# Half-array products of a decoder trunk gathered into longer sequences on TensorE

## The chip, the cores and the metric

The kernel runs on one core of a Trainium2 chip, written in Bass with the Tile framework. The metric is the device time of one execution in microseconds (us), the median over several runs. The engines are named as in the profile: PE is TensorE (matrix products; PEld is its weight load), DVE is VectorE, ACT is ScalarE, POOL is GpSimd, SP is SyncE, which issues the DMAs. PE multiplies with an array of 128 x 128 cells. A product that contracts over 64 rows, or that has 64 output columns, uses half of it.

## What is computed

Two layers of a decoder trunk over 256 positions of width 1024, in float32. Each layer normalizes x, projects it with `w_in`, runs three groups of heads next to each other, joins them with one output projection, adds the residual, and then does the same with a SwiGLU feed-forward network (FFN). The parts that the change touches are the retention (6 heads of width 64, chunks of 128 positions) and the weighted values of the sparse attention (NSA, 6 heads):

```python
def retention(q, k, v, g):
    ...
    scores = jnp.einsum('bhcnd,bhcmd->bhcnm', qc, kc) * decay[:, None]
    inner = jnp.einsum('bhcnm,bhcme->bhcne', scores, vc)
    ...
    o = rms_norm(o) * jax.nn.silu(g.astype(f32))

# nsa: compressed, selected and window branch, each a softmax over its keys
        o_c = jnp.einsum('bghqn,bgnd->bghqd', p_c, v_cmp)
        o_s = jnp.einsum('bghqk,bgqkd->bghqd', p_s, vs)
        o_w = jnp.einsum('bghqk,bgkd->bghqd', p_w, vw)
        return g[..., 0:1] * o_c + g[..., 1:2] * o_s + g[..., 2:3] * o_w

    x = x + (mix @ w_out[l])
```

## The kernel before

**Precision.** The large projections run as three products in the format fp32r: every weight piece comes by DMA into a staging tile `wst` (3 of them), ACT casts it to `whi` (6 tiles), and DVE subtracts that from the original to give `wlo` (6 tiles). A piece of `whi` and `wlo` is free again when PE has used it last; only then can the next cast into it begin, and a `wst` tile is free for the next DMA when its `wlo` is made. Small products in the heads are plain fp32; each stands in the trace as two records of PE.

**The order of work.** The kernel is written as threads (Python generators) that yield operations, wait for events or ask a pool for a tile. A planner, `Desk`, runs the threads against assumed costs while the program is built, and always issues the request that can start first, with priorities among those that can. The order that comes out is fixed: every engine works through its own instructions in that order, and an instruction whose inputs are not ready holds up all that stand behind it on the same engine. A list of operations yielded at once is issued without anything else of that engine between them.

**Pools.** PSUM has 8 banks: four `acc` for the projections and four `sm` for everything small (transposes, scores, sums). `S` has 4 tiles in SBUF for weighted scores.

**A layer, in order.** The projection is done in seven parts (`nk`, `nq`, `gm`, `nv`, `rq`, `rk`, `rg`), and the heads' threads start as their parts are done, so their small products are mixed in between the records of the later parts (`acc<-whi,hcat` and `acc<-wlo,hcat`, 384 columns wide in the last part, `rg`, the gate of the retention).

- Weighted values, `pv` (L1059): a thread for each j of 3, each with the two heads of both key groups g. It waits for the values `Vt`, the compressed probabilities `pcT` and the four softmax units that it uses, takes one `sm` bank, and yields 9 products: one of the compressed branch (`sm<-pcT,vbd`, 96 rows, full array), then 8 with 64 output columns each (`sm<-PT,V`, half of the array by columns; the two of g = 0 and 1 go to the two halves). Then `split` casts the bank on ACT (`nsh`) and subtracts on DVE (`nsl`).
- Retention, `retention` (L1159): three threads `scores(p)`, one for each pair of heads. Each takes two `S` tiles and two `sm` banks and yields two lists of two products that contract over 64 rows (`sm<-qkT`, half of the array by rows; the two heads lie on the two halves), 256 and 128 columns wide. For each head DVE then multiplies both parts with the decay (`S<-sm,cst`). The main thread takes, head by head, the 6 products of that head's sums (`sm<-rv,S`, 64 output columns, half of the array by columns) into two `sm` banks.
- `ret_norm` (L1209) squares the sums on ACT (`w2k<-sm`), reduces them on DVE, takes the inverse root by Ln and Exp on ACT, and scales (`ro`); `rg_tile` (L1222) multiplies with Silu of the gate, transposes on PE (`sm<-cst,ro`) and splits the result into `rth` and `rtl`. Silu and Ln/Exp need different tables of ACT.
- The output projection, `residual` (L1366), uses gm, then ns, then rt operands (`acc<-whi,gmh`, ..., `acc<-whi,rth`).

In the rows L196 is the line of the helper that records every operation, so operations are told apart by their tiles.

Of the kernel before, what the change touches and what calls it, by code (L numbers as in the profile page):

```python
# [258 lines left out]
class Desk:  # L259
# [33 lines left out]
    def give(self, pool, item):  # L293
        self.given += 1
        pool.free.append((self.cur.t, self.given, item))
        self._serve(pool)
# [94 lines left out]
class Trunk:  # L391
# [479 lines left out]
    def mix_nv(self, l, ps):  # L871
        self.gx = self.tiny("gx", [128, 2, 18])
        for t in range(2):
            self.desk.fork(self.nv_tile(l, t, ps[t]), 12)
        self.desk.fork(self.gates(l), 11)
        self.desk.fork(self.compress(l), 14)
        for h in range(0, 6, 2):
            self.desk.fork(self.unit(0, h), 18)
        for h in (0, 3, 1, 4, 2, 5):
            self.desk.fork(self.unit(1, h), 16)  # L880
        for j in range(3):
            self.desk.fork(self.pv(l, j), 9)

    def nv_tile(self, l, t, ps):
        V, A = self.V, self.A
# [22 lines left out]
    def compress(self, l):  # L908
# [6 lines left out]
        for j in range(2):  # L915
# [33 lines left out]
            self.vmask[:, :, None].to_broadcast([96, 6, 64]), op=ALU.mult,  # L949
        )  # L950
        give(self.sm, pv)

        pk = yield Need(self.sm)
# [102 lines left out]
        for i in range(m):  # L1056
            self.desk.fire(self.ev_u[t, h + i])

    def pv(self, l, j):  # L1059

        for t in range(2):
            yield self.ev_v[t]
        yield self.ev_pc
        for t in range(2):
            for g in range(2):
                yield self.ev_u[t, 3 * g + j]
        mm = self.PE.matmul
        po = yield Need(self.sm)
        ops = [
            mm(  # L1070
                po[:, :256], self.vbd[:, 2 * j : 2 * j + 2, :].rearrange("p g d -> p (g d)"), self.pcT,
                start=True, stop=False,
            )
        ]
        for b in range(2):
            for kt in range(2):
                qs = slice(128 * kt, 256)
                ks = slice(0, 256) if kt == 0 else slice(256, 384)
                for g in range(2):
                    vs = slice(b * 128 + g * 64, b * 128 + g * 64 + 64)  # L1080
                    ops.append(
                        mm(
                            po[64 * g : 64 * g + 64, qs], self.Vt[kt][:, vs], self.PT[:, 6 * b + 3 * g + j, ks],
                            start=False, stop=b == 1 and kt == 1,
                        )
                    )
        yield ops
        yield from self.split(self.nsh[j], self.nsl[j], po[:, :256])
        self.desk.give(self.sm, po)
        self.desk.fire(self.ev_ns[j])  # L1090


    def rope(self, src, dst, nh, t):
# [65 lines left out]
    def retention(self, l):  # L1159
        PE, V, give = self.PE, self.V, self.desk.give  # L1160
        for t in range(2):
            for e in (self.ev_rq[t], self.ev_rk[t], self.ev_rv[t][0], self.ev_rv[t][1]):
                yield e
        at = {}
        done = [Event() for _ in range(6)]


        def scores(p):
            yield self.ev_dec
            heads = []  # L1170
            for r in (0, 64):
                at[2 * p + r // 64] = a = yield Need(self.S)
                ps = yield Need(self.sm)
                heads.append((a, ps, self.qkT[r : r + 64, 3 + p, :], self.qkT[r : r + 64, p, :]))
            yield [PE.matmul(ps[:, :256], kT[:, :128], qT, start=True, stop=True) for _, ps, kT, qT in heads]
            yield [
                PE.matmul(ps[:, 256:384], kT[:, 128:], qT[:, 128:], start=True, stop=True) for _, ps, kT, qT in heads
            ]
            for h, (a, ps, _, _) in zip((2 * p, 2 * p + 1), heads):
                yield [  # L1180
                    V.tensor_tensor(a[:, :256], ps[:, :256], self.dec[:, h, :], op=ALU.mult),
                    V.tensor_tensor(a[:, 256:384], ps[:, 256:384], self.dec[:, h, :128], op=ALU.mult),
                ]
                give(self.sm, ps)
                self.desk.fire(done[h])

        for p in range(3):
            self.desk.fork(scores(p))
        po = []
        for h in range(6):  # L1190
            yield done[h]
            if h == 0:
                for t in range(2):
                    p = yield Need(self.sm)
                    po.append(p)
            hs = slice(h * 64, h * 64 + 64)
            a = at[h]
            yield [
                PE.matmul(
                    po[q][r : r + 64, hs], a[:, c + r : c + r + 64], self.rv[k][:, hs], start=k == 0, stop=k == q  # L1200
                )
                for q, k, c in ((0, 0, 0), (1, 0, 128), (1, 1, 256))
                for r in (0, 64)
            ]
            give(self.S, a)
        for t in range(2):
            self.desk.fork(self.ret_norm(t, po[t]))

# [407 lines left out]
```

## Time and profile before

| | us |
|---|---|
| median of 3 runs | 645.78 (645.46 to 646.02) |
| the profiled execution, its own time | 646.46 |
| its span, first to last instruction | 644.70 |
| PE busy | 635.1 (99%) |
| DVE busy | 452.9 (70%) |
| ACT busy | 364.8 (57%) |
| DMA, from HBM | 109.64 MB, 172 GB/s over the span |

A busy PE in this profile is one with a record open; records overlap in the pipeline, so the share says that PE was given work without a break, and the distance between the starts of neighbouring records says how fast it went. The chain that ended last lies on PE for 89% of the span and on DMAs for 5%.

### The profile page before, as it was taken

To read this page: it belongs to the slowest core of one execution; us is meant where nothing else is said; L and a number is where in the kernel's file an instruction comes from. 1 tells how busy PE (TensorE), PEld (TensorE's weight loads), DVE (VectorE), ACT (ScalarE), POOL (GpSimd) and SP (SyncE) were. 2 spreads that over 40 slices of the span, in tenths; PEclk is the share of its full clock that TensorE was granted. 3 is DMA by queue.
4 is the path that set the end of the run, shared out by engine and by line. 5 is a ranking of instruction groups with operands and counts; after the bars stand their busy time and mean duration, and the time that the engine had idled before them with its cause. 6 is when DMAs were issued, how large, how long until landed. Compare 5 with 4: busy or idle time off the path is not lost.

```text
span 644.7 us, 9955 instructions
## 1 busy us (share of the span) xinstructions
PE 635.1 (99%) x3628; PEld 533.6 (83%) x3628; DVE 452.9 (70%) x1046; ACT 364.8 (57%) x685; POOL 11.0 (2%) x28
## 2 busy tenths in 40 slices
PE   8979999999999999999999999999999999999998
PEld 7768887788888888888887888788888888888886
DVE  5867988488677677664388899865867677776441
ACT  7648963576456555543377795444755555545330
POOL 0120000000000000010000000000000000000000
PEclk9999999999999999999999999999999999999999
DMA  8885245157555565566546522534665556565631
GB/s 257 284 228 175 91 123 181 66 166 231 190 180 192 185 196 192 185 257 204 163 135 196 196 92 64 173 110 149 186 191 185 193 195 187 174 197 184 192 114 65
DMA packets 32816, 111.63 MB, mean 173 GB/s; under 512 B 4339, under 2 KB 4851, under 8 KB 32512
## 3 DMA queue, kind: packets, MB, share of 16 engines
q1 hardware_dynamic: 32256, 109.86, 52.4%
q0 software_dynamic: 512, 1.14, 0.9%
q8 instruction: 28, 0.46, 0.3%
q14 instruction: 20, 0.16, 0.1%
HBM read 109.64 MB, written 1.35 MB: 172 GB/s over the span
## 4 chain that ended last, share of the span: by engine, by line
PE 89%; DMA 5%; ACT 2%; DVE 2%; issue 1%; SPq 0%; ACTq 0%
PE acc L196 60%; PE sm L196 29%; DMA wst<-in_wts_dram 5%; ACT whi L196 1%; DVE wlo L196 1%; DMA x<-in_x_dram 1%; DVE x L196 0%; SPq L196 0%; ACT w2k L196 0%; ACT L402 0%; ACT L196 0%; DVE Kl L196 0%; ACT Kh L196 0%; ACT hcat L196 0%; ACT w1k L196 0%
## 5 line engine op out<-in xcount | busy, mean ns | idle before, releaser
L196 DVE TENSOR_TENSOR wlo<-wst,whi 128x1024 fp32r<-128x1024 f32 (+3 forms) x204 | 245.0, 1202 | 140.8 <-ACT whi L196 139.6
L196 ACT CAST whi<-wst 128x1024 fp32r<-128x1024 f32 (+3 forms) x204 | 209.2, 1028 | 195.0 <-issue 49.7
L196 PE MATMUL acc<-whi,hcat 128*128 128x512 f32 (+2 forms) x512 | 141.2, 381 | 0.0
L196 PEld LDWEIGHTS acc<-whi,hcat 128*128 128x128 f32 x512 | 91.6, 189 | 15.0 <-issue 0.7
L196 PE MATMUL acc<-hcat,whi 128*128 128x512 f32 x320 | 101.2, 396 | 0.0
L196 PE MATMUL sm<-hcat,whi 128*128 128x512 f32 x320 | 99.7, 392 | 0.0
L196 PE MATMUL acc<-wlo,hcat 128*128 128x512 f32 (+2 forms) x256 | 80.6, 381 | 0.0
L196 PEld LDWEIGHTS sm<-hcat,whi 128*128 128x128 f32 x320 | 60.0, 188 | 14.2
L196 PEld LDWEIGHTS acc<-hcat,wlo 128*128 128x128 f32 x320 | 58.8, 188 | 11.7
L196 PE MATMUL sm<-hcat,wlo 128*128 128x256 f32 x320 | 64.4, 282 | 0.0
L196 PE MATMUL acc<-hcat,wlo 128*128 128x256 f32 x320 | 64.1, 282 | 0.0
L196 PEld LDWEIGHTS acc<-wlo,hcat 128*128 128x128 f32 x256 | 46.8, 189 | 7.8 <-issue 0.3
L196 PEld LDWEIGHTS acc<-hcat,whi 128*128 128x128 f32 x320 | 50.9, 190 | 1.7
L196 PE MATMUL acc<-whi,ah 128*128 128x512 f32 (+1 forms) x176 | 50.0, 378 | 0.0
L196 PE MATMUL acc<-whi,al 128*128 128x512 f32 (+1 forms) x176 | 50.0, 378 | 0.0
L196 PE MATMUL acc<-wlo,ah 128*128 128x512 f32 (+1 forms) x176 | 49.9, 377 | 0.0
L196 PEld LDWEIGHTS sm<-hcat,wlo 128*128 128x128 f32 x320 | 49.6, 190 | 0.0
L196 PEld LDWEIGHTS acc<-whi,ah 128*128 128x128 f32 x176 | 31.9, 188 | 5.5
L196 PEld LDWEIGHTS acc<-wlo,ah 128*128 128x128 f32 x176 | 31.8, 188 | 5.5
L196 PEld LDWEIGHTS acc<-whi,al 128*128 128x128 f32 x176 | 31.8, 188 | 5.5
L196 ACT ACTIVATE hcat<-sm,par 128x128 fp32r<-128x128 f32 x64 | 18.6, 379 | 9.2 <-PE sm L196 9.2
L196 DVE SCALAR_TENSOR_TENSOR hcat<-sm,par,hcat 128x128 fp32r<-128x128 f32 x64 | 18.5, 344 | 4.5 <-ACT hcat L196 4.5
(212 smaller groups left out, 726.6 us busy)
## 6 DMA issues: line engine op xcount, KB each, us to landing
wst<-in_wts_dram SPq DMA_DIRECT2D x186, 512.0 KB, 3.8
wst<-in_wts_dram SPq DMA_DIRECT2D x8, 384.0 KB, 3.0
w<-in_w_dram SPq DMA_DIRECT2D x2, 1024.0 KB, 7.0
wst<-in_wts_dram SPq DMA_DIRECT2D x4, 411.0 KB, 4.4
x<-in_x_dram SPq DMA_DIRECT2D x4, 256.0 KB, 5.3
wst<-in_wts_dram SPq DMA_DIRECT2D x4, 256.0 KB, 3.3
cst<-in_cst_dram SPq DMA_DIRECT2D x1, 768.0 KB, 5.3
B<-scr POOLq DMA_DIRECT2D x4, 192.0 KB, 6.2
```

The costliest lines, as they stand in the source:

```text
L196: return Op(self.name, lambda: fn(*a, **k), dur, table, lat, prio, banks)
```

## The change

`mix_nv` starts one thread `pv(l)` in place of three. It waits for all twelve units, takes three `sm` banks, and yields the three full-array products of the compressed branch in one list, and then three lists of 8 half-array products with a priority ahead of all other work; a small thread `finish(j)` splits each bank when its list is done. `retention` issues the scores of the first two pairs in one list, then, when all four heads have been multiplied with the decay, the scores of the third pair and the sums of heads 0 to 3 in one list, and then the sums of heads 4 and 5. The wait for the decay table moves ahead of it all. What is computed, and with which products, stays as it was.

```diff
@@ -878,8 +878,7 @@
             self.desk.fork(self.unit(0, h), 18)
         for h in (0, 3, 1, 4, 2, 5):
             self.desk.fork(self.unit(1, h), 16)
-        for j in range(3):
-            self.desk.fork(self.pv(l, j), 9)
+        self.desk.fork(self.pv(l), 9)
 
     def nv_tile(self, l, t, ps):
         V, A = self.V, self.A
@@ -1056,38 +1055,55 @@
         for i in range(m):
             self.desk.fire(self.ev_u[t, h + i])
 
-    def pv(self, l, j):
+    def pv(self, l):
+
 
         for t in range(2):
             yield self.ev_v[t]
         yield self.ev_pc
         for t in range(2):
-            for g in range(2):
-                yield self.ev_u[t, 3 * g + j]
+            for h in range(6):
+                yield self.ev_u[t, h]
         mm = self.PE.matmul
-        po = yield Need(self.sm)
+        pos = []
+        for j in range(3):
+            po = yield Need(self.sm)
+            pos.append(po)
         ops = [
             mm(
-                po[:, :256], self.vbd[:, 2 * j : 2 * j + 2, :].rearrange("p g d -> p (g d)"), self.pcT,
-                start=True, stop=False,
+                pos[j][:, :256], self.vbd[:, 2 * j : 2 * j + 2, :].rearrange("p g d -> p (g d)"), self.pcT,
+                start=True, stop=False, lat=False,
             )
+            for j in range(3)
         ]
-        for b in range(2):
-            for kt in range(2):
-                qs = slice(128 * kt, 256)
-                ks = slice(0, 256) if kt == 0 else slice(256, 384)
-                for g in range(2):
-                    vs = slice(b * 128 + g * 64, b * 128 + g * 64 + 64)
-                    ops.append(
-                        mm(
-                            po[64 * g : 64 * g + 64, qs], self.Vt[kt][:, vs], self.PT[:, 6 * b + 3 * g + j, ks],
-                            start=False, stop=b == 1 and kt == 1,
+        yield ops
+        done = [Event() for _ in range(3)]
+
+        def finish(j):
+            yield done[j]
+            yield from self.split(self.nsh[j], self.nsl[j], pos[j][:, :256])
+            self.desk.give(self.sm, pos[j])
+            self.desk.fire(self.ev_ns[j])
+
+        for j in range(3):
+            self.desk.fork(finish(j))
+        for j in range(3):
+            ops = []
+            for b in range(2):
+                for kt in range(2):
+                    qs = slice(128 * kt, 256)
+                    ks = slice(0, 256) if kt == 0 else slice(256, 384)
+                    for g in range(2):
+                        vs = slice(b * 128 + g * 64, b * 128 + g * 64 + 64)
+                        ops.append(
+                            mm(
+                                pos[j][64 * g : 64 * g + 64, qs], self.Vt[kt][:, vs],
+                                self.PT[:, 6 * b + 3 * g + j, ks],
+                                start=False, stop=b == 1 and kt == 1, lat=False, prio=-2,
+                            )
                         )
-                    )
-        yield ops
-        yield from self.split(self.nsh[j], self.nsl[j], po[:, :256])
-        self.desk.give(self.sm, po)
-        self.desk.fire(self.ev_ns[j])
+            yield ops
+            self.desk.fire(done[j], self.desk.LAT["PE"])
 
 
     def rope(self, src, dst, nh, t):
@@ -1161,21 +1177,25 @@
         for t in range(2):
             for e in (self.ev_rq[t], self.ev_rk[t], self.ev_rv[t][0], self.ev_rv[t][1]):
                 yield e
+        yield self.ev_dec
         at = {}
         done = [Event() for _ in range(6)]
 
 
-        def scores(p):
-            yield self.ev_dec
+        def open_pair(p):
             heads = []
             for r in (0, 64):
                 at[2 * p + r // 64] = a = yield Need(self.S)
                 ps = yield Need(self.sm)
                 heads.append((a, ps, self.qkT[r : r + 64, 3 + p, :], self.qkT[r : r + 64, p, :]))
-            yield [PE.matmul(ps[:, :256], kT[:, :128], qT, start=True, stop=True) for _, ps, kT, qT in heads]
-            yield [
+            return heads
+
+        def scores(heads):
+            return [PE.matmul(ps[:, :256], kT[:, :128], qT, start=True, stop=True) for _, ps, kT, qT in heads] + [
                 PE.matmul(ps[:, 256:384], kT[:, 128:], qT[:, 128:], start=True, stop=True) for _, ps, kT, qT in heads
             ]
+
+        def decay(p, heads):
             for h, (a, ps, _, _) in zip((2 * p, 2 * p + 1), heads):
                 yield [
                     V.tensor_tensor(a[:, :256], ps[:, :256], self.dec[:, h, :], op=ALU.mult),
@@ -1184,25 +1204,47 @@
                 give(self.sm, ps)
                 self.desk.fire(done[h])
 
-        for p in range(3):
-            self.desk.fork(scores(p))
+        def sums(heads):
+            for h in heads:
+                hs = slice(h * 64, h * 64 + 64)
+                for q, k, c in ((0, 0, 0), (1, 0, 128), (1, 1, 256)):
+                    for r in (0, 64):
+                        yield PE.matmul(
+                            po[q][r : r + 64, hs], at[h][:, c + r : c + r + 64], self.rv[k][:, hs],
+                            start=k == 0, stop=k == q,
+                        )
+
+        first = yield from open_pair(0)
+        second = yield from open_pair(1)
+        yield scores(first) + scores(second)
+        self.desk.fork(decay(0, first))
+        self.desk.fork(decay(1, second))
+        for h in range(4):
+            yield done[h]
+        third = []
+        ps3 = []
+        for r in (0, 64):
+            ps = yield Need(self.sm)
+            ps3.append(ps)
         po = []
-        for h in range(6):
+        for t in range(2):
+            p = yield Need(self.sm)
+            po.append(p)
+        third = [
+            (None, ps, self.qkT[r : r + 64, 5, :], self.qkT[r : r + 64, 2, :]) for r, ps in zip((0, 64), ps3)
+        ]
+        yield scores(third) + list(sums(range(4)))
+        for h in range(4):
+            give(self.S, at[h])
+        for i, h in enumerate((4, 5)):
+            at[h] = yield Need(self.S)
+            third[i] = (at[h], *third[i][1:])
+        self.desk.fork(decay(2, third))
+        for h in (4, 5):
             yield done[h]
-            if h == 0:
-                for t in range(2):
-                    p = yield Need(self.sm)
-                    po.append(p)
-            hs = slice(h * 64, h * 64 + 64)
-            a = at[h]
-            yield [
-                PE.matmul(
-                    po[q][r : r + 64, hs], a[:, c + r : c + r + 64], self.rv[k][:, hs], start=k == 0, stop=k == q
-                )
-                for q, k, c in ((0, 0, 0), (1, 0, 128), (1, 1, 256))
-                for r in (0, 64)
-            ]
-            give(self.S, a)
+        yield list(sums((4, 5)))
+        for h in (4, 5):
+            give(self.S, at[h])
         for t in range(2):
             self.desk.fork(self.ret_norm(t, po[t]))
 
```

What this does to the order shows at three places. First PE in layer 0 at the weighted values, as a piece of the difference between the two programs (`V_0_131` and `V_0_132` are the values of the two halves of the positions):

```order
 L196 MATMUL acc_64<-wlo_83,hcat 128x384
 L196 MATMUL sm_68<-pcT_135,vbd_134 128x256
+L196 MATMUL sm_67<-pcT_135,vbd_134 128x256
+L196 MATMUL sm_70<-pcT_135,vbd_134 128x256
 L196 MATMUL sm_68<-PT_133,V_0_131 64x256 x2
 L196 MATMUL sm_68<-PT_133,V_0_132 64x128 x2
 L196 MATMUL sm_68<-PT_133,V_0_131 64x256 x2
 L196 MATMUL sm_68<-PT_133,V_0_132 64x128 x2
-L196 MATMUL sm_67<-pcT_135,vbd_134 128x256
 L196 MATMUL sm_67<-PT_133,V_0_131 64x256 x2
 L196 MATMUL sm_67<-PT_133,V_0_132 64x128 x2
```

The second full-array product moves from between two half-array strings to ahead of them; the third does the same.

Second PE in layer 1, in the retention: the sums of heads 0 to 2 before, each head between full-array products of the gate's projection or scores (`acc`; one `S` tile for each head).

```order
L196 MATMUL sm_67<-rv_1_2929,S_1_2935 64x64 x2
L196 MATMUL sm_69<-rv_1_2929,S_1_2935 64x64 x2
L196 MATMUL sm_69<-rv_1_2930,S_1_2935 64x64 x2
L196 MATMUL acc_63<-whi_76,hcat 128x384
L196 MATMUL acc_64<-whi_76,hcat 128x384
L196 MATMUL sm_67<-rv_1_2929,S_1_2936 64x64 x2
L196 MATMUL sm_69<-rv_1_2929,S_1_2936 64x64 x2
L196 MATMUL sm_69<-rv_1_2930,S_1_2936 64x64 x2
L196 MATMUL acc_63<-whi_77,hcat 128x384
L196 MATMUL acc_64<-whi_77,hcat 128x384
```

And the same heads on PE after the change, which follow the third pair's scores:

```order
L196 MATMUL sm_69<-qkT_2931 128x128
L196 MATMUL sm_70<-qkT_2931 128x128
L196 MATMUL sm_68<-rv_1_2929,S_1_2935 64x64 x2
L196 MATMUL sm_67<-rv_1_2929,S_1_2935 64x64 x2
L196 MATMUL sm_67<-rv_1_2930,S_1_2935 64x64 x2
L196 MATMUL sm_68<-rv_1_2929,S_1_2936 64x64 x2
L196 MATMUL sm_67<-rv_1_2929,S_1_2936 64x64 x2
L196 MATMUL sm_67<-rv_1_2930,S_1_2936 64x64 x2
L196 MATMUL sm_68<-rv_1_2929,S_1_2937 64x64 x2
L196 MATMUL sm_67<-rv_1_2929,S_1_2937 64x64 x2
```

The gate's products have gone from between the heads: 16 of them now stand between the first scores and the third, 10 between the sums of heads 0 to 3 and those of 4 and 5, and 8 behind these.

Third ACT in layer 1, from the squares of the sums (`w2k<-sm`) to the retention's result (`rth`). Before:

```order
L196 ACTIVATE w2k_91<-sm_67 128x384
L196 ACTIVATE w2k_92<-sm_69 128x384
L196 CAST whi_77<-wst_74 128x1024
L196 ACTIVATE rtr_z<-rtr_ss 128x6 x2
L196 ACTIVATE rtr_y<-rtr_z 128x6
L196 CAST whi_78<-wst_75 128x1024
L196 ACTIVATE rtr_y<-rtr_z 128x6
L196 CAST whi_79<-wst_73 128x1024
L196 ACT_TABLE_LOAD
L196 ACTIVATE w2k_89<-acc_63,rstd_110 128x384
L196 ACTIVATE w2k_90<-acc_64,rstd_111 128x384
```

After:

```order
L196 ACTIVATE w2k_88<-sm_68 128x384
L196 ACTIVATE w2k_92<-sm_67 128x384
L196 CAST whi_79<-wst_73 128x1024
L196 ACTIVATE rtr_z<-rtr_ss 128x6 x2
L196 ACT_TABLE_LOAD
L196 ACTIVATE w2k_93<-acc_63,rstd_110 128x384
L196 ACTIVATE w2k_90<-acc_64,rstd_111 128x384
L402 ACT_TABLE_LOAD
L196 ACTIVATE rtr_y<-rtr_z 128x6 x2
```

Silu of the gate (`w2k<-acc,rstd`) and its table now stand between Ln (`rtr_z`) and Exp (`rtr_y`), with a second table load; a further one follows at the start of layer 1's FFN, as the table is no longer that of Silu there. In layer 0 Silu moves the other way, ahead of the squares.

## Rows read from the trace of the kernel before

**Rows 1.** The page's first part: busy time of each engine in us (share of the span) x instructions.

```profile
PE 635.1 (99%) x3628; PEld 533.6 (83%) x3628; DVE 452.9 (70%) x1046; ACT 364.8 (57%) x685; POOL 11.0 (2%) x28
```

**Rows 2.** Who waited for whom, PE alone, longest first: us in total, times, longest. The list has four lines; the other two name x (0.3) and Kl (0.2).

```profile
PE sm L196 <- DVE w2k L196: 4.9, 2, 3.5
PE sm L196 <- DMA x<-in_x_dram: 0.8, 1, 0.8
```

**Rows 3.** Busy time of each engine in two stretches (us from the span's start; length, then PE, PEld, DVE, ACT, POOL with their instructions, the granted clock of PE, the DMA share, GB/s).

```profile
98.60:119.10 20.50, 20.50 (x195) 14.32 (x194) 14.18 (x40) 7.01 (x12) 0.00 (x0) 1.00 0.42 144
408.70:430.80 22.10, 22.10 (x203) 16.33 (x203) 14.66 (x39) 8.56 (x17) 0.00 (x0) 1.00 0.31 100
```

**Rows 4.** The timeline of PE around sums of layer 0: start us, length from the first start to the last end, what, number of records. The rows with x10 and x4 are the same string seen in narrower windows, from its third and from its ninth record on.

```profile
111.49 0.57 PE L196 MATMUL sm<-rv,S 128*64 128x64 f32 x12
111.60 0.46 PE L196 MATMUL sm<-rv,S 128*64 128x64 f32 x10
111.77 0.29 PE L196 MATMUL sm<-rv,S 128*64 128x64 f32 x4
...
117.67 0.34 PE L196 MATMUL acc<-wlo,hcat 128*128 128x384 f32 x1
117.93 0.57 PE L196 MATMUL sm<-rv,S 128*64 128x64 f32 x12
118.43 0.44 PE L196 MATMUL acc<-wlo,hcat 128*128 128x384 f32 x1
118.71 0.51 PE L196 MATMUL acc<-whi,hcat 128*128 128x384 f32 x2
119.06 0.63 PE L196 MATMUL acc<-whi,gmh 128*128 128x512 f32 x2
```

**Rows 5.** The timeline of PE in layer 1, where full-array records follow each other.

```profile
427.33 0.85 PE L196 MATMUL acc<-whi,hcat 128*128 128x384 f32 x4
428.03 0.51 PE L196 MATMUL acc<-wlo,hcat 128*128 128x384 f32 x2
```

**Rows 6.** The timeline of PE in layer 1, a string of 8 score records in windows from its third, fifth and seventh record on, and what follows.

```profile
417.63 0.71 PE L196 MATMUL sm<-qkT 64*128 64x128 f32 x6
417.74 0.60 PE L196 MATMUL sm<-qkT 64*128 64x256 f32 x4
417.96 0.38 PE L196 MATMUL sm<-qkT 64*128 64x256 f32 x2
418.27 0.62 PE L196 MATMUL acc<-wlo,hcat 128*128 128x384 f32 x2
```

**Rows 7.** The timeline of PE in layer 0: the first weighted values (the row with x14 is the string of 16 from its third record on), the second pcT, and the gm products behind the third string.

```profile
98.64 0.62 PE L196 MATMUL sm<-pcT,vbd 96*128 96x256 f32 x2
99.19 1.52 PE L196 MATMUL sm<-PT,V 128*64 128x256 f32 x16
99.45 1.25 PE L196 MATMUL sm<-PT,V 128*64 128x256 f32 x14
100.64 0.70 PE L196 MATMUL sm<-pcT,vbd 96*128 96x256 f32 x2
105.30 1.06 PE L196 MATMUL sm<-gmv,wsT 128*128 128x128 f32 x8
```

**Rows 8.** Groups of PE's instructions by shape in the stretch from 98.6 to 119.1 us: xcount, busy us, mean ns of one, idle before.

```profile
L196 PE MATMUL acc<-whi,hcat 128*128 128x384 f32 x18 | 5.1, 366 | 0.0
L196 PE MATMUL acc<-wlo,hcat 128*128 128x384 f32 x10 | 3.4, 369 | 0.0
L196 PE MATMUL sm<-PT,V 128*64 128x128 f32 x24 | 2.3, 273 | 0.0
L196 PE MATMUL sm<-cst,w1k 128*128 128x128 f32 x8 | 1.3, 287 | 0.0
L196 PE MATMUL sm<-gmv,wsT 128*128 128x128 f32 x8 | 1.1, 275 | 0.0
```

**Rows 9.** The timeline of PE earlier in layer 0: products of the key compression, also half of the array by columns, which the change leaves alone.

```profile
65.82 2.22 PE L196 MATMUL sm<-aT,w 128*64 128x33 f32 x64
```

**Rows 10.** The timeline of DVE in layer 0: a weight split, and the decay of two heads.

```profile
108.69 1.23 DVE L196 TENSOR_TENSOR wlo<-wst,whi 128x1024 fp32r<-128x1024 f32 x1
109.83 1.15 DVE L196 TENSOR_TENSOR S<-sm,cst 128x256 f32<-128x256 f32 x4
```

**Rows 11.** The timeline of ACT, DVE and PE in layer 0 along the retention's result: squares, table load, the products with Silu (two, the first done half way), transposes.

```profile
118.31 0.87 ACT L196 ACTIVATE w2k<-sm 128x384 f32<-128x384 f32 x2 [3.71 <-PE sm L196]
122.74 1.28 ACT L402 ACT_TABLE_LOAD   x1
126.05 1.01 DVE L196 TENSOR_TENSOR ro<-ro,w2k 128x384 f32<-128x384 f32 x2
127.27 0.49 PE L196 MATMUL sm<-cst,ro 128*128 128x128 f32 x3
```

**Rows 12.** The timeline of ACT in layer 1: a cast of weights, Ln, a table load, Silu.

```profile
426.88 1.05 ACT L196 CAST whi<-wst 128x1024 fp32r<-128x1024 f32 x1
427.84 0.30 ACT L196 ACTIVATE rtr_z<-rtr_ss 128x6 f32<-128x6 f32 x2
432.07 1.28 ACT L196 ACT_TABLE_LOAD   x1
433.37 1.05 ACT L196 ACTIVATE w2k<-acc,rstd 128x384 f32<-128x384 f32 x2
```

**Rows 13.** The timeline of ACT after layer 1's output projection; in brackets the idle time before and what ended it.

```profile
465.99 1.05 ACT L196 CAST whi<-wst 128x1024 fp32r<-128x1024 f32 x1 [2.23 <-DMA wst<-in_wts_dram]
```

## The prediction

> **What bounds the kernel now.** I read the engines' busy time first. TensorE (PE) is busy 635.1 of 644.7 us [rows 1]. A busy PE need not be a PE that gains from shorter work, so the waits come next: the list of who waited for whom, longest first, is down to 0.8 us at its second line for PE, and both lines belong to the start [rows 2]. In the two stretches that the change touches, the gathered products of layer 0 (98.6 to 119.1 us) and of layer 1 (408.7 to 430.8), PE is busy all the time, at a granted clock of 1.00, while VectorE (DVE) is busy for some two thirds and ScalarE (ACT) for a third [rows 3]. Time saved on PE there should come off the end, if nothing new keeps PE waiting.
>
> The timeline shows what can be saved. An fp32 product stands as two records, and two products on different halves of the array run side by side, so I count pairs of records. Inside a string of sums a pair follows the pair before after 0.17/3 = 0.057 us (111.60 to 111.77). The edges are slower. A full-array record of 384 columns takes 0.175 us in its own kind [rows 5]; the last one before a sums string takes 0.26 (117.67 to 117.93), the first sums pair 0.11, the last sums pair 0.16 (118.43 less 118.27, where four steps of 0.057 past the second pair put it), and the first full-array record after it 0.28 (118.43 to 118.71) [rows 4]. So going in costs 0.09 + 0.05 = 0.14 us and coming out 0.10 + 0.10 = 0.20. The scores show the same: 0.11 and 0.22 per pair inside the string, 0.31 for the last pair before a full-array record [rows 6].
>
> **The price of a change of shape.** For the mean over all kinds I take layer 0 as a balance: 119.06 - 98.64 = 20.42 us [rows 4, 7]. Its work at the pace inside strings: 26 full-array records of 384 columns (28 in the group view, two of which began before 98.64) at 0.175, 4.55; 8 transposes and 8 wsT records at (1.06 - 0.275)/7 = 0.112, 1.79 [rows 7, 8]; 6 pcT records of twice that width, 1.34; three weighted-value strings. The row from 99.45 has 6 steps, half of each width, in 1.25 - 0.27 = 0.98, so a string of 8 steps is 1.31 and three are 3.92 [rows 7, 8]. Three pairs of score heads at 2 x (0.22 + 0.11), 1.98; 36 sums pairs at 0.057, 2.05. Together 15.63, which leaves 4.79 us. In this stretch the program changes 27 times between full array, half by rows (scores, 64 of 128 rows) and half by columns (weighted values, sums): 0.177 us each. That lies between the 0.14 and 0.20 of the single edges, so nothing else is in the stretch, no wait above all.
>
> [...]
>
> **The change, part by part.** (1) Weighted values: the three pcT products move ahead, and 24 half-array products follow in one string. Per layer 6 changes become 2. The pace inside a longer string is the same if the 64-record string of 65.82 us is a guide: 2.22 us, 0.06 to 0.07 per pair to its end [rows 9]. Six pcT records in a row are not in the trace; they could cost up to 0.02 more each, as the first pair does (0.62 less one duration of 0.38 is 0.24 against 0.224 [rows 7]), or nothing: 0 to 0.1 us a layer; I take 0. (2) Scores and sums: layer 0 has 21 changes and keeps 7, layer 1 has 18 and keeps 7. (3) No product is added or dropped and no DMA is; on ACT two table loads of 1.28 us come in with layer 1. One stands in the chain of the retention's result (below); the other comes ahead of the first Silu of the FFN, whose first transposes the order now puts 17 rows later on PE, so it is covered.
>
> Removed: 27 + 24 - 9 - 9 = 33 changes. At 0.177 us: **5.8 us**; all at the cheap edge (0.14) 4.6, all at the dear one (0.20) 6.6. The mix removed is 12 entries by columns, 7 by rows and 14 returns to the full array, near the mean, so I keep 5.8 and allow 5.2 to 6.4.
>
> **What the longer strings wait for.** Each string now waits for all its inputs, and behind a waiting product stands every later product, as PE works in order. Three places.
> First, the sums of heads 0 to 3 need eight decay operations on DVE, 1.15 us for four, so 2.3, perhaps behind one weight split of 1.23 [rows 10]. Between the first scores and these sums PE has 17 full-array products in layer 0 (13 x 0.175 + 4 x 0.112 = 2.7) and 16 in layer 1 (2.8), and the third scores (0.66 and a change). That is 3.6 us against at most 3.5; DVE also starts while the second pair's scores run (0.66). No wait, margin about 0.7.
> Second, the sums of heads 4 and 5: ahead of them stand 24 pairs (1.4) and 8 or 10 full-array products (1.8), 3.2 us, against 1.15 to 2.4 on DVE. No wait.
> Third, the transposes of ro in the output projection. In layer 0 they keep their place in the order, while the last sums move behind 8 of the projection's products. From the last sums pair PE now arrives after 0.16 + 28 x 0.228 + 0.1 = 6.6 us (36 records take 8.21 from 119.06 to 127.27 [rows 4, 11]). The chain: squares 0.87, a table load 1.28, then 2.5 from its end to the first finished ro (124.02 to 126.55) [rows 11]: 4.7, since Silu and its table load now stand ahead of the squares on ACT. Margin 1.9. In layer 1 ACT's order is worse: from the last sums pair 8 products (1.7) finish the projection of the gate and free the weight tile, then a cast (1.05 as its neighbours), two Ln (0.30), a table load (1.28), Silu (1.05), a second table load (1.28) [rows 12], and the same 2.5 to ro: 9.2 us. PE arrives after 0.16 + 8 x 0.175 + 34 x 0.228 + 0.1 = 9.4. Margin 0.2, which one weight split on DVE (1.23) would turn into a wait of 1.0. I take 0 and keep 1.0 for the range.
>
> **Sum.** The profiled execution took 646.46 us, a span of 644.70 and 1.76 around it; less 5.8 is 640.6. The median of the runs is 645.78, 0.68 lower; less 5.8 is **639.9 us**.
>
> **Rivals.**
> A (my forecast): 5.2 to 6.4 us are gained, 639.4 to 640.6.
> B: PE waits at the new places. For it: the margin of 0.2 in layer 1, and that four score heads at once hold all four sm banks, which gm, the transposes and the next scores share. Against: the margins above. Price 1 to 3 us, 641 to 643. [...]
> C: the gain is given back. ACT waits up to 2.23 us for weights near 466 us [rows 13]; if the weight stream sets the pace there, PE comes early and stands until the old time: 645.8. Against: the casts of that stage wait first for tiles that PE frees, and these come earlier with PE; PE's own list holds no weight tile [rows 2].
> [...]
> That the program doesn't gather is excluded: its order shows the strings.
>
> **How the numbers follow.** A 0.78, B 0.13, C 0.05, D 0.04. Faster by over 0.2% (below 644.5; 0.2% is about what a measurement of this kernel can tell from no change): A and B, 0.91. Within: C, 0.05. Slower: D, 0.04. The range reaches from 639.1 (the edges dearer than their mean) to 642.8, most of B; it leaves out C, D and the ends of A and B, some 0.15.
>
> **What would show it.** In the changed profile: weighted-value strings of 48 records, starting 0.7 us earlier relative to the gm products; 24 pairs of sums in about 1.45 us; from the first pcT to the output projection's ninth product 19.1 us where 22.3 stood (20.42 + 8 x 0.228, less 18 x 0.177); PE without a wait ahead of ro. Wrong would be: pairs inside the long strings above 0.07 us, a wait of PE for S, for an sm bank or for ro, or a lower clock in the strings.

## The result, and the profile after

The changed kernel takes 640.02 us (median of 4 runs, 639.65 to 640.73) against 645.9 us beside it; the ratio is 0.991 with a 95% interval of 0.9893 to 0.9928. Forecast were 639.9 us and a range of 639.1 to 642.8. The profiled execution took 639.65 us, its span is 637.8.

The first part of its page, PE's busy time in us, share and instructions, answers to [rows 1]: 6.2 us less, and still 99%.

```profile
PE 628.9 (99%) x3628; PEld 534.1 (84%) x3628; DVE 452.5 (71%) x1046; ACT 367.4 (58%) x687; POOL 11.7 (2%) x28
```

Who waited for whom, PE alone: only the two waits of the start are left, as long as before [rows 2]. No S tile, no `sm` bank and no `ro` is among them.

```profile
PE sm L196 <- DVE w2k L196: 5.0, 2, 3.6
PE sm L196 <- DMA x<-in_x_dram: 0.8, 1, 0.8
```

The timeline of PE in layer 0 (start us, length, what, records), strings and what follows each:

```profile
98.62 1.49 PE L196 MATMUL sm<-pcT,vbd 96*128 96x256 f32 x6
100.03 4.12 PE L196 MATMUL sm<-PT,V 128*64 128x256 f32 x48
104.09 0.66 PE L196 MATMUL sm<-cst,w1k 128*128 128x128 f32 x4
...
113.14 1.62 PE L196 MATMUL sm<-rv,S 128*64 128x64 f32 x48
114.69 0.73 PE L196 MATMUL acc<-whi,gmh 128*128 128x512 f32 x2
...
117.59 0.73 PE L196 MATMUL acc<-wlo,gmh 128*128 128x512 f32 x2
...
124.07 0.49 PE L196 MATMUL sm<-cst,ro 128*128 128x128 f32 x3
```

Read two distances in it. From the first pcT to the transposes of ro are 124.07 - 98.62 = 25.45 us; before they were 127.27 - 98.64 = 28.63 [rows 7, 11]. That is 3.18 less for 18 changes of shape removed, 0.177 each. From the first pcT to the product behind the weighted values are 104.09 - 98.62 = 5.47. Layer 1, the same view:

```profile
405.22 1.48 PE L196 MATMUL sm<-pcT,vbd 96*128 96x256 f32 x6
...
410.68 1.10 PE L196 MATMUL sm<-cst,w1k 128*128 128x128 f32 x8
...
424.67 0.63 PE L196 MATMUL acc<-whi,gmh 128*128 128x512 f32 x2
...
431.96 0.63 PE L196 MATMUL acc<-wlo,gmh 128*128 128x512 f32 x2
432.43 0.82 PE L196 MATMUL sm<-cst,ro 128*128 128x128 f32 x6
```

And PE in layer 1 of the kernel before:

```profile
408.71 0.61 PE L196 MATMUL sm<-pcT,vbd 96*128 96x256 f32 x2
...
430.80 0.39 PE L196 MATMUL acc<-whi,gmh 128*128 128x512 f32 x1
```

From pcT to the output projection are 424.67 - 405.22 = 19.45 us, where 430.80 - 408.71 = 22.09 stood: 2.64 less for 15 changes, 0.176 each. The two stretches give 5.82. The medians show the gain of the whole only roughly: the interval of the ratio reaches from 4.7 to 6.9 us.

### The profile page after: what moved, and what is told of

It reads as the page before. It is cut to its first block, busy times and chain, and to the rows that moved or that the text cites. A ratio compares the mean times of both kernels' runs of the same rounds, so it can differ in the third digit from the quotient of the medians.

```text
span 637.8 us, 9961 instructions
## 1 busy us (share of the span) xinstructions
PE 628.9 (99%) x3628; PEld 534.1 (84%) x3628; DVE 452.5 (71%) x1046; ACT 367.4 (58%) x687; POOL 11.7 (2%) x28
## 4 chain that ended last, share of the span: by engine, by line
PE 96%; DMA 2%; DVE 1%; ACT 0%; SPq 0%; issue 0%
PE acc L196 67%; PE sm L196 29%; DMA wst<-in_wts_dram 1%; DMA x<-in_x_dram 1%; DVE wlo L196 0%; ACT whi L196 0%; SPq L196 0%; DVE w2k L196 0%; DVE x L196 0%; ACT w2k L196 0%; ACT Kh L196 0%; DVE nqr_y L196 0%
```

## The experiments

Theory 1 is that of the prediction: PE pays for each change of array shape, and whatever else the order does costs nothing. The rival: the gain comes from the places where products stand and what they wait for. In the table "median" is to be compared with the kernel before, measured beside it (646.4), and "changes" counts those between full array, half by rows and half by columns in the whole program (69 before).

| kernel | changes | median us | ratio (95%) |
|---|---|---|---|
| e1, weighted values only | 61 | 644.58 | 0.9971 (0.9960 to 0.9983) |
| e2, retention only | 44 | 640.93 | 0.9915 (0.9896 to 0.9933) |
| e3, extra products ahead | 36 | 643.75 | 0.9958 (0.9942 to 0.9974) |
| e4, the same between | 80 | 650.02 | 1.0066 (1.0047 to 1.0086) |
| e5, extra products ahead | 36 | 642.88 | 0.9955 (0.9938 to 0.9972) |
| e6, the same between | 66 | 648.61 | 1.0034 (1.0022 to 1.0047) |
| e7, retention in two strings | 30 | 639.00 | 0.9887 (0.9874 to 0.9900) |
| e8, small products full-array | 24 | 644.17 | 0.9968 (0.9956 to 0.9979) |
| e9, e7 and e8 | 18 | 642.88 | 0.9948 (0.9933 to 0.9963) |
| e10, the changed kernel | 36 | 640.30 | 0.9916 (0.9903 to 0.9930) |
| e11, e8 moved in SBUF | 24 | 642.16 | 0.9935 (0.9918 to 0.9952) |
| e12, the changed kernel moved | 36 | 642.59 | 0.9939 (0.9921 to 0.9956) |

**The halves of the change, e1 and e2.** Each has one of the two functions of the diff and the other as before.

> Only the weighted values are gathered, the retention is that of before: 61 changes of array shape are left of 69. Theory 1 (each change between full array, half by rows and half by columns costs PE 0.177 us, and nothing else matters): 8 x 0.177 = 1.4 us less than before, 644.5, ratio 0.998; each layer's stretch from the first pcT to the transposes of the gm products is 0.7 us shorter. Rival (the gain comes from the new places of the products in the order, in the retention above all, where they wait less for their inputs): no gain here, 645.9.

> Only the retention is gathered, the weighted values are those of before: 44 changes of shape are left of 69. Theory 1: 25 x 0.177 = 4.4 us less than before, 641.5, ratio 0.993. Rival (places in the order): the whole gain, 640.0, as the weighted values were not waiting for anything. If e1 and e2 together give more or less than the whole change by over 0.5 us, the two parts are not independent.

PE in layer 0 of e1, then of e2, from the first pcT:

```profile
98.32 1.49 PE L196 MATMUL sm<-pcT,vbd 96*128 96x256 f32 x6
...
103.79 0.66 PE L196 MATMUL sm<-cst,w1k 128*128 128x128 f32 x4
...
126.25 0.49 PE L196 MATMUL sm<-cst,ro 128*128 128x128 f32 x3
```

```profile
99.37 0.62 PE L196 MATMUL sm<-pcT,vbd 96*128 96x256 f32 x2
...
105.54 0.66 PE L196 MATMUL sm<-cst,w1k 128*128 128x128 f32 x4
...
125.51 0.49 PE L196 MATMUL sm<-cst,ro 128*128 128x128 f32 x3
```

The weighted values take 5.47 us gathered (e1) and 6.17 not (e2): 0.70 for 4 changes, 0.175 each. From there to ro are 22.46 us with the old retention and 19.97 with the new: 2.49 for 14 changes, 0.178 each. In the changed kernel both new numbers stand side by side (5.47, then 124.07 - 104.09 = 19.98), so in this stretch the parts are independent to 0.01 us. The medians don't show that: 1.9 and 5.5 less than before make 7.4, against 5.9 for the whole, which is over the 0.5 us that were set as the sign of parts that depend on each other; and e2's 640.93 lies between the two forecasts. The decision rests on the stretches: in e1 a part that never waited gains in proportion to its changes, and there the rival falls.

**The price alone, e3 to e6.** Extra products do nothing but change the shape, ahead of a string (no change added) or inside it.

```diff
+        self.zero = self.fixed("zero", [128, 128], F32R)
...
+        mm(pos[j][:, :128], self.zero, self.zero, start=False, stop=False)
...
+        PE.matmul(heads[0][1][:, 384:512], self.zero, self.zero, start=True, stop=True)
```

> The changed kernel with 11 more full-array products a layer (weights of zeros, 128 columns, added to the banks of the weighted values, which they leave as they are), all ahead of the string of weighted values. No change of shape is added. It is the base for the next kernel. All theories: 22 products at 0.05 to 0.11 us (the pace of full-array records of 128 columns) more than the changed kernel, 641.1 to 642.4.

> The same 11 products a layer, now one between every two steps of the string, so that PE changes its shape 44 times more; the order on every engine is else the same but for two casts' neighbours on DVE. Theory 1: 44 x 0.177 = 7.8 us more than the kernel with the products ahead (6.2 at the cheap edges, 0.14; 7.5 at 0.14 in and 0.20 out). Rival (what counts is where products stand and what they wait for, as these wait for nothing): the same time as with the products ahead, within 1 us.

PE in layer 0 of e3, then of e4:

```profile
99.67 1.46 PE L196 MATMUL sm<-pcT,vbd 96*128 96x256 f32 x6
100.78 1.53 PE L196 MATMUL sm<-zero 128*128 128x128 f32 x11
...
106.29 0.44 PE L196 MATMUL sm<-cst,w1k 128*128 128x128 f32 x2
```

```profile
99.06 1.46 PE L196 MATMUL sm<-pcT,vbd 96*128 96x256 f32 x6
...
101.03 0.33 PE L196 MATMUL sm<-zero 128*128 128x128 f32 x1
101.29 0.44 PE L196 MATMUL sm<-PT,V 128*64 128x128 f32 x4
101.66 0.33 PE L196 MATMUL sm<-zero 128*128 128x128 f32 x1
...
108.99 0.44 PE L196 MATMUL sm<-cst,w1k 128*128 128x128 f32 x2
```

From pcT to the product behind are 6.62 us with the products ahead and 9.93 with them between: 3.31 for 22 changes, 0.150 each, and the medians differ by 6.3 us for 44. The extra products wait for nothing, and the order is otherwise the same, so the rival (within 1 us) falls. But 0.177 was too much here: 7.8 were expected, and a round trip is 3.31/11 = 0.30 us, not the 0.34 of [rows 4]. One step of e4 shows where that lies. From one extra product to the next are 101.66 - 101.03 = 0.63 us: 0.26 for the extra product, whose own pace is 0.105 ((6.62 - 5.47)/11), and 0.37 for two pairs of 0.11. So 0.15 stand on each side. On the half-array side that is what [rows 4] has (0.05 + 0.10); the full-array side would be 0.10 + 0.09 there. The extra product has 128 columns, and a return to such a product is cheaper, alone or not. PE in the changed kernel, from the second w1k record behind the string of weighted values on, and in the kernel before the second pcT record behind a string:

```profile
104.25 0.49 PE L196 MATMUL sm<-cst,w1k 128*128 128x128 f32 x3
104.58 1.06 PE L196 MATMUL sm<-gmv,wsT 128*128 128x128 f32 x8
105.39 0.94 PE L196 MATMUL acc<-whi,hcat 128*128 128x384 f32 x4
106.17 0.35 PE L196 MATMUL acc<-wlo,hcat 128*128 128x384 f32 x1
```

```profile
100.96 0.38 PE L196 MATMUL sm<-pcT,vbd 96*128 96x256 f32 x1
```

The first of four w1k records takes 104.25 - 104.09 = 0.16 us where the next take 0.11, so 0.05 more; the first pcT, of 256 columns, 100.96 - 100.64 = 0.32 [rows 7] where 0.22 is its pace, so 0.10 more. With 0.05 in place of 0.10 the full-array side is 0.14, which is what e4 has but for 0.01.

The rows of the changed kernel also answer a rival that was not tested by itself: every half-array product here is fp32 and most of their neighbours are fp32r, so the price could be that of the format. From the eight gmv records (fp32) to behind the four hcat records (fp32r), all on the full array, are 106.17 - 104.58 = 1.59 us; at their own paces, 8 x 0.112 + 4 x 0.175, they make 1.60. So a change of format alone costs nothing here.

> The changed kernel with 8 more full-array products a layer (weights of zeros, 128 columns, into unused columns of the score banks), all ahead of the scores' strings. No change of shape is added. Base for the next kernel: 16 products at 0.05 to 0.11 us more than the changed kernel, 640.8 to 641.8.

> The same 8 products a layer, now between the pairs of scores, between the third scores and the sums and between the heads' sums: 30 changes of shape more (16 of them at scores, 14 at sums), the order on every engine else the same. Theory 1: 30 x 0.177 = 5.3 us more than with the products ahead. Rival: within 1 us of it.

PE in layer 0 of e5 and of e6, from a full-array record ahead of the third scores to the output projection:

```profile
115.50 0.52 PE L196 MATMUL acc<-whi,hcat 128*128 128x384 f32 x2
115.85 0.67 PE L196 MATMUL sm<-zero 128*128 128x128 f32 x5
...
118.85 0.50 PE L196 MATMUL acc<-whi,gmh 128*128 128x512 f32 x1
```

```profile
114.11 0.34 PE L196 MATMUL acc<-whi,hcat 128*128 128x384 f32 x1
...
116.44 0.33 PE L196 MATMUL sm<-zero 128*128 128x128 f32 x1
116.70 0.57 PE L196 MATMUL sm<-rv,S 128*64 128x64 f32 x12
...
118.71 0.50 PE L196 MATMUL acc<-whi,gmh 128*128 128x512 f32 x1
```

The extra products are the rows of `zero`, five in one place in e5, one by one between the heads' sums in e6. Here 118.85 - 115.50 less one step of 0.175 (two records against one at the start) is 3.18, and 118.71 - 114.11 is 4.60: 1.42 for 9 changes, 0.158 each. The medians of the whole differ by 5.7 us for 30, 0.19 each. Scores and sums pay as the weighted values do.

The two kernels with the products ahead missed their own forecasts: e3 is 1.3 us above the upper end (642.4), e5 1.1 (641.8). The copy that fills `zero` changes the order at the start, on PE from its thirteenth record on. The first key compression product (`sm<-aT,w`) starts at 67.44 us in e3 and 69.66 in e5, 65.80 in the changed kernel. From there to the end of the span are 574.4 and 573.3 us, against 572.0: 2.4 more for 22 products and 1.3 for 16, 0.11 and 0.08 each. The lower pace of 0.05 us in both expectations is shown by no run: the extra products of e3 follow each other at 0.105.

**More of the same, e7 to e10.** e7 gathers the third pair's scores with the first two and all six heads' sums.

```diff
-        yield scores(first) + scores(second)
+            at[4 + r // 64] = a = yield Need(self.w2k)
+            ps = yield Need(self.acc)
...
+        yield scores(first) + scores(second) + scores(third)
...
-        yield scores(third) + list(sums(range(4)))
+        yield list(sums(range(6)))
```

> The retention in two strings a layer: the scores of all three pairs in one (the third pair in two acc banks), the sums of all six heads in one. 30 changes of shape are left of the 36 of the changed kernel. Theory 1: 6 x 0.177 = 1.1 us less than the changed kernel, 6.9 less than before, ratio 0.989. Rival (longer strings wait for their inputs): the sums of layer 0 need twelve decay operations, 3.5 us on DVE, against some 1.3 (the second and third pair's scores) + 2.7 us of PE work between; one weight split of 1.2 us in between makes a wait of up to 0.7 a layer, and the time is that of the changed kernel or 0.3 us more.

PE in layer 1 of e7:

```profile
409.94 1.10 PE L196 MATMUL sm<-cst,w1k 128*128 128x128 f32 x8
...
423.35 0.63 PE L196 MATMUL acc<-whi,gmh 128*128 128x512 f32 x2
```

From the product behind the weighted values to the output projection are 13.41 us, 13.99 in the changed kernel (424.67 - 410.68): 0.58 for 3 changes, 0.19 each. No wait for a decay appears, so the rival's reason falls. It is the fastest kernel here, 1.3 us below e10, which was measured beside it, with intervals that don't overlap. The two profiled executions don't show that this gain is the strings': their spans differ by 1.0 us (636.9 and 637.9), but e7 is 1.15 ahead at the first key compression product already (64.99 us, 66.14 in e10), up to where the order is the same, and from there to the end the two take 571.9 and 571.8 us. So what layer 1's stretch gains is lost again elsewhere in this execution. PE waits 0.4 us for x in e7's list and not in e10's; as the list of the kernel before has such a wait too (0.3), no run shows that the strings bring it.

e8 takes lone half-array products away by padding.

```diff
-        yield PE.matmul(pv[:96, :64], hv.rearrange("p j c -> p (j c)"), self.w2[64:, :], start=True, stop=True)
+        yield PE.matmul(pv[:, :64], hg, self.w2, start=True, stop=True)
...
-        yield PE.matmul(pk[:32, :64], hk, self.w2[:64, :], start=True, stop=True)
...
-        yield self.transpose(pt[:, :32], kd.rearrange("p r d -> p (r d)"))
+        yield self.transpose(pt[:, :128], kd)
```

> Three lone small products a layer of the key compression made full-array ones by padding with zeros: the two products with w2 (64 rows each) become one of 128 rows, and the transpose of its result (32 rows) becomes one of 128 rows. 24 changes of shape are left of 36, and one product a layer less. Theory 1: 12 x 0.177 = 2.1 us less than the changed kernel, 7.9 less than before, ratio 0.988. Rival (a full-array product costs twice the half one, and what a lone product costs is its own pipeline, not the shape): within 0.5 us of the changed kernel.

> Both of the above, 18 changes of shape left of 36. Theory 1: 18 x 0.177 = 3.2 us less than the changed kernel, 9.0 less than before, ratio 0.986. Rival: as in the two parts, 0.991.

> The changed kernel itself, beside the three others on the same chip. All theories: 5.8 less than before, ratio 0.991.

e10 came out as expected. e8 missed by 6.0 us: it has 12 changes fewer than the changed kernel and is 3.9 us slower than e10, where 2.1 less were expected. e9 missed by 5.8 and is slower than e10 too. The traces of both show one cause that has nothing to do with shapes: PE's records in the down projections, far from the edit, run slower. Their tiles lie 128 bytes further in SBUF, because the two new padded tiles are larger than those that they replace. The last two kernels test this.

**The place in SBUF, e11 and e12.** An unused tile of 384 bytes (e11, on e8) or 128 bytes (e12, on the changed kernel):

```diff
+        self.fixed("pad", [128, 96])
```

> The kernel with the three small products made full-array, and an unused tile of 384 bytes a partition ahead of the tiles of the layers, so that these lie 512 bytes further than in the changed kernel instead of 128 (the order on every engine is the same as without it). Layout theory (the 0.232 us per record in its down projections in place of 0.227 come from where the tiles lie): 0.227 us per record there again, layer 0's down projection 61.0 us for 62.4, and 12 x 0.177 = 2.1 us less than the changed kernel, 638.2, ratio 0.988. Rival (the padding itself costs it, by the order it gives): 62.4 us again, 644, ratio 0.997.

> The changed kernel with an unused tile of 128 bytes a partition ahead of the tiles of the layers and nothing else; the order is the same on every engine. Layout theory: layer 0's down projection takes 62.4 us for 61.0, and the whole 2 to 3 us more than the changed kernel, 642.2 to 643.2. Rival: no change, 640.2, ratio 0.991.

The down projection of layer 0: PE's instructions that read `ah` (min, median and max duration in ns, first and last start), in e10, e12, e8 and e11:

```profile
L196 PE MATMUL acc<-whi,ah x88: 387/389/476, 264.4 to 325.0; 128*128 128x512 f32 x88
```

```profile
L196 PE MATMUL acc<-whi,ah x88: 390/393/477, 264.8 to 326.7; 128*128 128x512 f32 x88
```

```profile
L196 PE MATMUL acc<-whi,ah x88: 390/393/477, 264.3 to 326.3; 128*128 128x512 f32 x88
```

```profile
L196 PE MATMUL acc<-whi,ah x88: 387/389/481, 265.5 to 326.1; 128*128 128x512 f32 x88
```

From the first to the last start: 60.6 us in e10, 61.9 in e12, 62.0 in e8, 60.6 in e11. So 128 bytes cost about 1.3 us there, with nothing else changed in e12, and 512 bytes cost nothing. In layer 1's down projection the same distance is 59.6 us in e10 (573.2 to 632.8) and 60.2 in e12 (575.7 to 635.9), another 0.6. The layout theory holds for this stage, in both layers. For the whole, e12 is 2.3 us above e10 by the medians, which is what was expected, but their intervals overlap.

It explains only part of e8. e11 has the old pace and is 2.0 us faster than e8, but still 1.9 us above e10, where 2.1 less were expected. PE at the padded products in e11:

```profile
76.89 0.60 PE L196 MATMUL sm<-cst,S 128*128 128x128 f32 x4
77.33 0.42 PE L196 MATMUL sm<-w,hgz 128*128 128x64 f32 x2
77.55 0.48 PE L196 MATMUL sm<-Kh,Q 128*128 128x512 f32 x1
...
85.79 0.33 PE L196 MATMUL sm<-cst,kdz 128*128 128x128 f32 x1 [0.42 <-DVE kdz L196]
...
392.28 0.44 PE L196 MATMUL sm<-cst,S 128*128 128x128 f32 x2 [0.21 <-DVE S L196]
392.91 0.30 PE L196 MATMUL sm<-cst,kdz 128*128 128x128 f32 x1 [0.19 <-DVE kdz L196]
```

The padded product is entered without a price (77.33 is four steps of 0.11 behind 76.89) and takes 0.22. So the shape's price is gone at this product, and PE now waits for DVE's chain at the transpose behind it, 0.6 us of PE in all by the list of waits, and 0.2 for S. Besides, of the 1.7 us between the spans of the two profiled executions (639.6 and 637.9), 1.5 lie ahead of the first key compression product (67.61 us in e11, 66.14 in e10). That part moves without any change of shape too (69.66 in e5, 64.99 in e7). Behind that product the two take the same time, 572.0 and 571.8 us: the 2.1 us of theory 1 are missing there in full, and what e8's rival said of the whole, within 0.5 us of the changed kernel, is what this execution shows. e11's two added memsets change the order at the start, on PE from its fifth record on; whether they set the 1.5, and what took the gain beyond the waits, stays open.

## Why the prediction was right

**PE bounds, and nothing new waits.** Right: the list of waits after has the two lines of the start and no other. The chain that ended last lies on PE for 96% of the span, for 89% before.

**The price of a change of shape.** Right as a mean: 0.177 was read from layer 0's balance, and e1 and e2 gave 0.175 and 0.178 in separate stretches, the changed kernel 0.177 and 0.176 in the two layers. 33 changes make 5.82 us in the two stretches, for 5.8. The mean belongs to this mix, though. It was carried over to e4, where PE returns to products of 128 columns, and there a change costs 0.150. That the median of the whole comes within 0.1 us of the forecast is partly luck, as it is known to about 1 us only. The traces show that a change costs, in e4 with nothing to wait for (3.31 us for 22), and split the price over the records on both sides of the change (of e4's round trip of 0.30 us, 0.15 on each). What PE does in that time no run shows.

**The work inside the strings.** The weighted values' stretch is 0.70 us shorter in each layer, so six pcT records in a row cost nothing more that shows; I had taken 0 with up to 0.1 a layer. The long string of sums takes 114.69 - 113.14 = 1.55 us for 24 pairs, where the list of signs said about 1.45: that number had left out the 0.10 of the return. From pcT to the ninth product of the output projection are 117.59 - 98.62 = 18.97 us, for 19.1.

**Where the strings wait (rival B).** They don't. The tightest margin was ro in layer 1, 0.2 us by the sum. ACT and DVE there, and PE at 432.43 above:

```profile
426.18 1.28 ACT L196 ACT_TABLE_LOAD   x1
...
428.55 1.28 ACT L402 ACT_TABLE_LOAD   x1
```

```profile
431.62 1.01 DVE L196 TENSOR_TENSOR ro<-ro,w2k 128x384 f32<-128x384 f32 x2
```

The second of the two DVE products starts about half way (432.09), so the first ro is done near 432.1; PE comes to the transposes two steps of 0.228 behind 431.96, at 432.42, and goes on at 432.43. The margin was some 0.3 us. Both table loads stand in the chain, as forecast, and are hidden.

**The gain given back (rival C).** No: the time came off the end. **The clock (rival D, a lower granted clock in the strings).** No. The stretches of the longest strings, with PE's busy time, its granted clock and the DMA share in the last columns:

```profile
100.00:104.10 4.10, 4.10 (x50) 3.02 (x49) 4.06 (x12) 1.79 (x3) 0.00 (x0) 1.00 0.73 228
113.10:114.70 1.60, 1.60 (x51) 1.49 (x49) 1.60 (x3) 1.58 (x2) 0.00 (x0) 1.00 0.12 18
```

The clock stays at 1.00 through 4.1 us of half-array products. A lower one is in the same trace, 0.50 from 48.0 to 51.0 us, far ahead of these stretches (in the kernel before from 47.5 to 50.5); so a drop would show in this column, and in these strings there is none. What one would cost them no run shows.

**What the sum did not hold.** The two profiled executions differ by 646.46 - 639.65 = 6.81 us, one more than the stretches explain; the medians differ by 5.9 (6.1 beside e10). The one before lies 0.6 above its median (645.9) and the one after 0.4 below its own, so the medians leave nothing over. Of the one, 0.3 is gained between layer 0's ro (3.20 ahead) and layer 1's pcT (408.71 - 405.22 = 3.49 ahead), the rest behind the start of layer 1's output projection, where the wait of PE for x in the list before (0.3 us) stands that is gone after. The wait for Kl is gone too, but plays no part: behind it, at the first key compression product, the two are level (65.82 and 65.80).

## What to carry to other kernels

Where PE is the bound, count how often neighbouring products differ in array shape, read the price from one string with its edges, and take count times price for the same mix of products: here 0.175 to 0.178 us a change, 0.150 to 0.158 where PE returned to products of 128 columns. Before gathering, sum up when every input of the longer string is ready; all margins held here, the smallest by some 0.3 us. Count the gain at the end and not in the stretch alone: e11 took twelve more changes away, PE waited for DVE for a part of what they should have given, and its profile shows no gain. After any edit that adds or resizes a tile, compare the pace of the large products far from the edit before the edit is judged.

## What the runs showed of the hardware

A move of the tiles by 128 bytes a partition slowed PE's products in layer 0's down projection from 60.6 to 61.9 us (389 to 393 ns median a record), a move by 512 bytes did not (60.6 in e11); e8 and e12, with different programs, show the same (62.0 and 61.9). In e12 the order on every engine is that of e10, so the tiles' place alone slowed PE there. What in the address sets the pace no run here shows. The price of a change of shape is split over the records on both sides of it (0.15 us on each for a round trip in e4), and depends on the product that PE returns to: the first record behind a half-array string took 0.05 us more than its pace with 128 columns, 0.10 more with 256.
